# The squares of the first norm: eight instructions between the split parts, or two wide ones behind them

## The chip, the cores and the metric

The kernel runs on one core of a Trainium2 chip. The metric is the device time of one execution in microseconds (us), the median of the runs of a kernel. The core's engines are TensorE (PE; its weight loads are shown apart as PEld), VectorE (DVE), ScalarE (ACT), GpSimd (POOL) and SyncE (SP, which here only issues DMAs). Each takes its instructions in the order in which they were laid down, and waits where an operand is not ready.

## What is computed

One pre-norm layer over x, 512 tokens of 1024 channels, in float32, and a final RMS norm:

```
h    = rmsnorm(x, norm1_g)
proj = h @ w_in                     # parts for four mixers, and four gates of 1024 columns
ys   = gated DeltaNet, RG-LRU, S5, RWKV-7, each from its part of proj
x    = x + (sum_i sigmoid(gate_i) * (ys[i] @ w_branch[i])) @ w_out
h2   = rmsnorm(x, norm2_g)
x    = x + square(relu(h2 @ mlp_w1)) @ mlp_w2
out  = rmsnorm(x, final_norm_g)
```

The part that matters here is the first line: `rmsnorm` divides each token's channels by the root of their mean square (plus 1e-6), times a weight per channel.

## The kernel before

x lies transposed in SBUF: eight chunks of 128 channels by 512 tokens, side by side in one tile `xt` (`xt0`, which fills the region c1b). Its eight loads are issued by SP (line 251) between the raw weights of the first projection and those of the second.

**Products.** A float32 product is done in three matmuls of a reduced format: each operand is split in a high part and the low rest. For x that is `split_g` (line 382), per chunk: ACT scales by the norm's weight and rounds to the high part (line 117), DVE makes the low part (line 129). Weights come in *units* of 128x1024 (`unit`, line 316): the load of `raw` by SP (line 313), the high part by ACT (`hi<-raw`, line 117), the low part by DVE (`lo<-raw,hi`, line 120). Four raw buffers and two of each part are in turn. `gemm` (line 337) then runs 24 matmuls of 128x512 for a unit: for each of the eight chunks high by high, high by low, low by high. The trace calls these `acc<-c,hi` and `acc<-c,lo`.

**The norm.** The projections use x before it is divided; the scale per token, `rsa`, is applied when a projection leaves PSUM (`nproj`, line 419). The scale comes from `norm_stat` (line 345). ACT squares each chunk (`act(sq, xt[k], ACT.Square)`), DVE adds the squares as they come, TensorE sums over the 128 channels of a partition (`ssa`, matmuls with a column of ones), ACT takes the root, DVE the reciprocal, TensorE spreads the result over the partitions (`rsa`), ACT copies it out. The first six projections have a PSUM bank each, so six can be done before one must be scaled.

```
 408          for k in range(8):
 409              split_g(xs[k], "g1", k, xgh[:, k, :], xgl[:, k, :])
 410          N1["rs"] = norm_stat(xs, "a")
 411          fr(xt)
```

**The order of the work.** No order is written out by hand. Each step of a list `PLAN` is emitted at a priority number of its level (`LV`, `level`); units have lower numbers, which rank first, by line 320: `100 * u - (30000 if u else 50000)`. A planner with its own timeline of the kernel (`schedule_with_timeline_sim=True`, line 1816) puts each engine's instructions in line: of those that it holds ready, the one that ranks first. The DMA queue of SP is such a line too. The order is then fixed; the chip only waits.

**Places in SBUF.** Small tiles share five regions: c0 (for the split x), c1a, c1b, c2 and c3. `al` (line 138) gives a tile the place that the table `HOME` names for its name and turn, if that is free at that point of the program; otherwise it searches the free place whose last user was released longest ago. An instruction that writes a tile waits on the chip for the readers of what lay there before.

Other names in the text: `omu` and the activations `c<-pr`, `ea<-pr`, `cl<-pr` prepare constants of the mixers from the parameters `pr` (its second load is line 254); `zero` is a tile of zeros that SP writes eight times to scratch memory (line 432); `wt`, `s5p` and `cb` are a decay table of RWKV, powers for S5 and a constant matrix; `zpg` and `t1pr` are steps of an inversion of triangular blocks in two mixers.

Of the kernel before, what the change touches and what calls it, by code (L numbers as in the profile page):

```python
# [22 lines left out]
HOME = {n: [(a[:a.index(":")], int(a[a.index(":") + 1:])) for a in v.split(",")] for n, v in (e.split("=") for e in """
    xt0=c1b:0 xgh=c0:0 xgl=c0:128 sqa0=c3:650 sqa1=c3:64 sqa2=c3:333 sqa3=c3:618 sqa4=c3:558 sqa5=c1a:81 sqa6=c3:634
    sqa7=c2:185 rsa=c3:202 zero=c2:43,c1b:78 wa=c3:514 gd=c3:64
    px=c2:52,c2:205,c3:383,c3:112,c3:218,c1a:105,c1b:0,c3:488,c3:526,c1b:16,c3:298,c1b:112,c3:525,c1b:16,c2:0,c1b:16
    reset=c3:542 kr=c1b:32 yk=c2:178 svr=c3:0 ab=c2:43 ccb=c1a:59 kf=c3:96,c1a:17 sig=c1b:96,c3:112 af=c3:466,c1b:96
    ei=c1b:112,c1a:0 eia=c1a:80,c3:558 wt=c1a:63,c3:447 bigwup=c3:325 hsbk=c1b:16,c3:298 rf=c3:80,c3:423
    vf=c3:333,c1b:112 rb=c3:349,c3:321 ntr=c1a:64 a2=c3:439 biggup=c2:242 s5s=c3:314 s5pol=c3:134 s5p=c1a:41
    bst=c1a:33 bsx=c2:8 bs2=c3:610 bs3=c3:530 c1=c1a:51 c2=c2:0 bigsb=c3:234 bigsbs=c3:666 bigsc=c2:16 bigscs=c1a:97  # L30
    b8=c3:358 s5t=c3:218,c3:610 s5u=c1a:96 s5ug=c3:325 s5h=c1a:0 lrow=c3:509 gsm=c2:250 ctri=c3:504 qk=c3:96,c3:391
    cv=c1b:0,c3:542,c1b:0,c1b:96,c1a:32,c1a:32 gv=c3:359 lu=c3:542 lh=c1b:96 lr=c1b:0,c1b:16 li=c3:509,c1b:0
    la2=c3:298,c3:298 biglwa=c2:27 biglwx=c2:35 lge=c3:526,c1b:16 c8=c3:218 t8w=c3:138 s5ct=c3:574 s5st=c3:590
    s5am=c2:18 s5ph=c2:175 s5tb=c3:282 s5a=c3:540 s5b=c3:503 s5hs=c3:290 cmr=c3:606 tfr=c2:0 bk=c3:610 s5y=c3:513
    s5yf=c3:326 s5yo=c3:514 bigglu=c1a:48 sgm=c3:290,c3:306 nbr=c1b:87 tnr=c3:128 tmr=c1b:70 tpr=c1b:32 t0tr=c2:210
    ztr=c1b:32 t11tr=c3:574 z2r=c1a:32 ktok=c2:176 ksqg=c1b:64 gpk=c3:136 grows=c3:130 gr=c1a:64 br=c1a:96 eg=c1a:0
    cneg=c2:173 cmg=c2:171 kx=c1b:64 kd=c3:250 svg=c2:176 aq=c3:546 tw=c3:324 ntg=c1a:0 tfg=c3:291 nbg=c1a:40
    tng=c2:35 tmg=c1a:112 tpg=c1a:32 t0tg=c1a:80 ztg=c1a:32 t11tg=c1a:64 z2g=c1a:112
    gt=c1b:0,c1b:0,c1b:16,c3:178,c1b:16,c3:178,c1b:16,c1b:16,c1b:0,c1b:48,c1b:16,c3:185,c1b:16,c1b:16,c3:170,c2:59,c3:234,c1b:0,c3:218,c3:610,c1b:0,c1b:48,c2:75,c2:176,c3:32,c2:0,c3:186,c1b:96,c2:42,c3:513,c1b:16,c2:125,c3:23,c2:32,c3:610,c3:626,c1b:0,c3:580,c3:598,c3:626,c3:337,c3:16,c3:136,c3:64,c3:594,c3:80,c3:626,c3:317
    ofr=c3:128 r1=c3:282,c1b:0,c1b:48,c3:194,c1b:40,c1b:40,c3:505,c1b:40  # L40
    uv=c1b:48,c1b:40,c1b:56,c3:503,c3:168,c3:160,c3:177,c2:34
    sm=c1b:8,c3:194,c1b:40,c3:185,c3:503,c3:168,c3:160,c1b:56 ofg=c2:143
    sn=c3:282,c3:473,c2:117,c3:282,c3:160,c1b:32,c2:92,c3:316
    sgs=c1b:32,c1b:40,c1b:75,c3:315,c3:473,c1b:75,c3:282,c1b:88 osq=c3:658,c3:626 hsbv=c2:16,c3:16 yh1=c1a:32
    yl1=c1a:64 mg=c3:456,c3:497,c3:170,c3:0,c3:48,c3:481,c3:658,c3:234 yh2=c1a:0 yl2=c1a:96 gz=c3:64 q2=c3:530,c1b:112
    o2=c2:240,c3:186 hsbo=c1b:96,c3:513 yh3=c1a:64 yl3=c1a:32 yh0=c1a:96 yl0=c1a:0
    x2=c3:107,c3:642,c3:423,c3:388,c3:407,c3:372,c3:439,c3:290 mh=c2:0 ml=c2:128 h2h=c0:0 h2l=c0:128 sqb0=c3:64
    sqb1=c3:610 sqb2=c3:32 sqb3=c3:0 sqb4=c3:16 sqb5=c3:48 sqb6=c3:531 sqb7=c3:626 rsb=c3:332
    dh=c1a:0,c1b:0,c2:128,c2:0 dl=c2:128,c2:0,c1a:0,c1b:0
    rl=c3:658,c3:0,c3:573,c3:626,c3:20,c3:46,c3:255,c3:0,c3:626,c3:0,c3:594,c3:16,c3:32,c3:56,c3:0,c3:16,c3:16,c3:626,c3:0,c3:32,c3:16,c3:626,c3:156,c3:658,c3:626,c3:610,c3:594,c3:503,c3:626,c3:16,c3:658,c3:0  # L50
    hc0=c3:497 hc1=c3:578 hc2=c3:184 hc3=c3:626 hc4=c3:658 hc5=c3:200 hc6=c3:481 hc7=c3:34 sqc0=c3:513 sqc1=c3:610
    sqc2=c3:236 sqc3=c3:16 sqc4=c3:533 sqc5=c3:610 sqc6=c3:562 sqc7=c3:594 rsc=c3:0
""".split())}
# [47 lines left out]
def trunk(ctx, tc, order, xT, wall, w8, prm, big, cst, gfr, out):  # L101
    nc = tc.nc
    V, A, G, P = nc.vector, nc.scalar, nc.gpsimd, nc.tensor
# [9 lines left out]
    def mm(o, l, r, start=True, stop=True):  # L113
        P.matmul(out=o, lhsT=l, rhs=r, start=start, stop=stop)  # L114

    def act(o, i, f, scale=1.0, bias=0.0):
        A.activation(out=o, in_=i, func=f, scale=scale, bias=bias)  # L117

    def tt(e, o, a, b, op):
        e.tensor_tensor(out=o, in0=a, in1=b, op=op)  # L120
# [99 lines left out]
    def pa(name):  # L220

        n = turn["acc"] = turn.get("acc", -1) + 1
        if n < EARLY or turn.get("late"):
# [4 lines left out]
        return pacc.tile([128, 512], F, tag=f"acc{n % 3}", name=name)


    def v3(t, a):
# [56 lines left out]
    one = const.tile([128, 1], F, name="one")  # L288
    G.memset(one, 1.0)
    ones = bc(one, [128, 128])  # L290
    with priority(-70000):
        o = ps("warm")
# [49 lines left out]
                mm(o, a[:, k0 + k, :], b[:, k, :], first and n == 0, last and n == 3 * nk - 1)  # L342
                n += 1

    def norm_stat(xt, nm, parts=1):

        accs = []
        for k in range(8):
            sq = t2(f"sq{nm}{k}")
# [9 lines left out]
        def keep_warm(n, t):
            if parts > 1:  # L360
                w = pa("warm")
                for _ in range(n):
                    mm(w[:, 0:128], ones, t[:, 0:128])
# [2 lines left out]
        for i, acc in enumerate(accs):
            for u in range(4):
                mm(o[:, u:u + 1], acc[:, u * 128:u * 128 + 128], one, i + u == 0, i == parts - 1 and u == 3)
            keep_warm(3, acc)
        fr(*accs)  # L370
# [1451 lines left out]
```

## Time and profile before

| what | value |
|---|---|
| median of 3 runs | 883.51 us (882.94 to 1213.66) |
| the profiled execution, its own time | 878.68 us |
| its span, first to last instruction | 876.9 us |
| TensorE busy | 855.5 us |
| VectorE busy | 549.2 us |
| ScalarE busy | 422.8 us |
| GpSimd busy | 26.1 us |
| TensorE's granted clock, mean | 0.991 |

All views that follow are of the profiled execution; starts are microseconds from the beginning of its span. A timeline row has start, length, engine, line of the kernel, operation, output and inputs by the program's names, shapes, count, and in brackets the idle time of the engine just before with what ended it. Tiles that lie in a region show as the region's name: `c<-c1b` writes some tile of c and reads x. A wait row has the engine and instruction that waited, what for, the total in us, how often, and the longest. A group row ends with busy time and the mean length in ns, then idle time ahead. Instructions on one engine overlap a little at their ends, so the distance between two starts is what one costs its engine.

### The profile page before, as it was taken

To read this page: it belongs to the slowest core of one execution; us is meant where nothing else is said; L and a number is where in the kernel's file an instruction comes from. 1 tells how busy PE (TensorE), PEld (TensorE's weight loads), DVE (VectorE), ACT (ScalarE), POOL (GpSimd) and SP (SyncE) were. 2 spreads that over 40 slices of the span, in tenths; PEclk is the share of its full clock that TensorE was granted. 3 is DMA by queue.
4 is the path that set the end of the run, shared out by engine and by line. 5 is a ranking of instruction groups with operands and counts; after the bars stand their busy time and mean duration, and the time that the engine had idled before them with its cause. 6 is when DMAs were issued, how large, how long until landed. Compare 5 with 4: busy or idle time off the path is not lost.

```text
span 876.9 us, 12992 instructions
## 1 busy us (share of the span) xinstructions
PE 855.5 (98%) x5175; PEld 688.8 (79%) x5175; DVE 549.2 (63%) x967; ACT 422.8 (48%) x584; POOL 26.1 (3%) x38
## 2 busy tenths in 40 slices
PE   8999999998999899999999999999999999999996
PEld 6777777777777787777888788888888888888885
DVE  6899796993776258636655652454437553868553
ACT  8735557854522273333433333765545443644433
POOL 1000000000000000000000000000100110010000
PEclk9999999999999799999999999999999999999999
DMA  8433345455465652244323232556665877463302
GB/s 296 135 107 110 108 112 116 96 154 150 123 178 151 180 171 73 83 134 117 96 92 102 77 131 96 192 145 173 164 194 159 246 169 200 159 137 104 120 25 96
DMA packets 79292, 119.96 MB, mean 137 GB/s; under 512 B 42544, under 2 KB 49392, under 8 KB 79216
## 3 DMA queue, kind: packets, MB, share of 16 engines
q1 hardware_dynamic: 51968, 100.40, 35.4%
q0 software_dynamic: 3456, 12.58, 8.3%
q10 hardware_dynamic: 23808, 6.16, 3.3%
q8 instruction: 40, 0.66, 0.3%
q14 instruction: 20, 0.16, 0.1%
HBM read 103.79 MB, written 13.17 MB: 133 GB/s over the span
## 4 chain that ended last, share of the span: by engine, by line
PE 79%; DVE 7%; DMA 7%; ACT 4%; issue 2%; SPq 1%; ACTq 0%; DVEq 0%
PE acc L114 24%; PE facc L114 20%; PE dacc L114 17%; PE oacc L114 5%; PE bacc L114 4%; DVE c L120 2%; DMA c1a<-scrg 1%; DVE lo L120 1%; DMA c1a<-gscr 1%; ACT c L117 1%; PE s L114 1%; DMA raw<-in_wall_dram 1%; DVE c L129 1%; ACT L117 1%; DVE c1a L120 1%
## 5 line engine op out<-in xcount | busy, mean ns | idle before, releaser
L114 PE MATMUL acc<-c,hi 128*128 128x512 f32 x864 | 278.3, 400 | 3.7 <-DVE c L129 2.5
L117 ACT ACTIVATE hi<-raw 128x1024 fp32r<-128x1024 f32 x113 | 119.4, 1058 | 239.0 <-PE facc L114 73.5
L120 DVE TENSOR_TENSOR lo<-raw,hi 128x1024 fp32r<-128x1024 f32 x113 | 137.9, 1221 | 118.4 <-ACT hi L117 118.3
L114 PEld LDWEIGHTS acc<-c,hi 128*128 128x128 f32 x864 | 161.6, 190 | 44.4 <-DVE c L129 5.0
L114 PE MATMUL acc<-c,lo 128*128 128x512 f32 x432 | 173.9, 404 | 1.4 <-DVE lo L120 1.4
L114 PE MATMUL facc<-c,hi 128*128 128x512 f32 x336 | 103.4, 389 | 0.0
L114 PEld LDWEIGHTS acc<-c,lo 128*128 128x128 f32 x432 | 81.9, 190 | 20.6 <-DVE lo L120 2.0
L114 PEld LDWEIGHTS facc<-c,hi 128*128 128x128 f32 x336 | 63.1, 188 | 13.1
L117 ACT ACTIVATE c<-c 128x512 f32<-128x512 f32 (+5 forms) x101 | 63.9, 638 | 18.5 <-DVE c L120 11.8
L120 DVE TENSOR_TENSOR c<-c 128x16 f32<-128x16 f32 (+8 forms) x125 | 65.1, 534 | 4.2 <-ACT c L117 3.8
L114 PE MATMUL facc<-c,lo 128*128 128x512 f32 x168 | 65.5, 390 | 0.0
L114 PE MATMUL facc<-c,c1a 128*128 128x512 f32 x264 | 62.8, 391 | 0.0
L114 PE MATMUL dacc<-hi,c 128*128 128x512 f32 x176 | 57.4, 389 | 0.0
L114 PEld LDWEIGHTS facc<-c,c1a 128*128 128x128 f32 x264 | 49.3, 188 | 10.1
L117 ACT ACT_TABLE_LOAD x41 | 52.6, 1283 | 8.5 <-DMA raw<-in_wall_dram 3.0
L120 DVE TENSOR_TENSOR c<-acc,c 128x512 f32<-128x512 f32 x33 | 22.6, 687 | 45.4 <-PE acc L114 45.1
L120 DVE TENSOR_TENSOR c1a<-raw,c1a 128x1024 fp32r<-128x1024 f32 x21 | 25.7, 1223 | 32.7 <-ACT c1a L117 32.6
L114 PE MATMUL bacc<-c1a,hi 128*128 128x512 f32 x128 | 40.6, 401 | 0.0
L114 PE MATMUL oacc<-c,hi 128*128 128x512 f32 x128 | 39.8, 392 | 0.1
L117 ACT ACTIVATE c1a<-raw 128x1024 fp32r<-128x1024 f32 x21 | 22.2, 1058 | 36.5 <-PE facc L114 29.0
L114 PEld LDWEIGHTS dacc<-hi,c 128*128 128x128 f32 x176 | 33.0, 188 | 6.8
L114 PEld LDWEIGHTS facc<-c,lo 128*128 128x128 f32 x168 | 31.5, 188 | 6.5
(390 smaller groups left out, 1194.4 us busy)
## 6 DMA issues: line engine op xcount, KB each, us to landing
raw<-in_wall_dram SPq DMA_DIRECT2D x134, 512.0 KB, 3.5
c<-in_wall_dram POOLq DMA_DIRECT2D x18, 512.0 KB, 5.7
c<-in_wall_dram SPq DMA_DIRECT2D x6, 512.0 KB, 3.5
raw<-in_wall_dram POOLq DMA_DIRECT2D x6, 512.0 KB, 7.1
scg<-c1b SPq DMA_DIRECT2D x11, 256.0 KB, 2.5
c<-scg SPq DMA_DIRECT2D x11, 256.0 KB, 3.6
c1b<-in_xT_dram SPq DMA_DIRECT2D x8, 256.0 KB, 5.2
c<-in_xT_dram SPq DMA_DIRECT2D x8, 256.0 KB, 4.0
```

Of the source, the lines that this page charges most:

```text
L114: P.matmul(out=o, lhsT=l, rhs=r, start=start, stop=stop)
L117: A.activation(out=o, in_=i, func=f, scale=scale, bias=bias)
L120: e.tensor_tensor(out=o, in0=a, in1=b, op=op)
L129: V.scalar_tensor_tensor(out=o, in0=a, scalar=s, in1=b, op0=op0, op1=op1)
```

## The change

`norm_stat` takes the whole tile of x. Two instructions square four chunks each, the even ones (0, 2, 4, 6) and the odd ones, each into a tile of 2048 columns; one addition of 2048 columns joins them, then one of 1024 and one of 512 fold the rest. The four column sums are those of before. The variable number of parts and the optional matmuls around it, unused for this norm, are gone.

```diff
-    def norm_stat(xt, nm, parts=1):
-
-        accs = []
-        for k in range(8):
-            sq = t2(f"sq{nm}{k}")
-            act(sq, xt[k], ACT.Square)
-            if k == 0 or k == 7:
-                accs.append(sq)
-            else:
-                tt(V, accs[-1], accs[-1], sq, ADD)
-                fr(sq)
-        while len(accs) > parts:
-            tt(V, accs[-2], accs[-2], accs[-1], ADD)
-            fr(accs.pop())
...
+    def norm_stat(xt, nm):
+
+
+        sq_ = [t8(f"sw{nm}{e}") for e in range(2)]
+        sq = [v3(t, 4) for t in sq_]
+        for e in range(2):
+            act(sq[e], v3(xt, 8)[:, e:8:2], ACT.Square)
+        tt(V, sq_[0], sq_[0], sq_[1], ADD)
+        fr(sq_[1])
+        for n in (1024, 512):
+            tt(V, sq_[0][:, 0:n], sq_[0][:, 0:n], sq_[0][:, n:2 * n], ADD)
         o = ps("ss" + nm)
...
+        for u in range(4):
+            mm(o[:, u:u + 1], sq_[0][:, u * 128:u * 128 + 128], one, u == 0, u == 3)
+        fr(sq_[0])
...
-        N1["rs"] = norm_stat(xs, "a")
+        N1["rs"] = norm_stat(xt, "a")
```

The table `HOME` is set anew for many small tiles; the wide squares, `swa0` and `swa1`, have no entry in it. The lines of the first tiles (a number counts 32 columns from the region's start):

```diff
-    xt0=c1b:0 xgh=c0:0 xgl=c0:128 sqa0=c3:650 sqa1=c3:64 sqa2=c3:333 sqa3=c3:618 sqa4=c3:558 sqa5=c1a:81 sqa6=c3:634
-    sqa7=c2:185 rsa=c3:202 zero=c2:43,c1b:78 wa=c3:514 gd=c3:64
+    xt0=c1b:0 xgh=c0:0 xgl=c0:128 sqa0=c3:212 sqa1=c3:17 sqa2=c3:250 sqa3=c3:290 sqa4=c1b:57 sqa5=c3:332 sqa6=c3:642
+    sqa7=c1a:4 rsa=c3:202 zero=c1b:96,c1a:31 wa=c3:514 gd=c3:64
...
-    reset=c3:542 kr=c1b:32 yk=c2:178 svr=c3:0 ab=c2:43 ccb=c1a:59 kf=c3:96,c1a:17 sig=c1b:96,c3:112 af=c3:466,c1b:96
+    reset=c3:594 kr=c1b:32 yk=c2:178 svr=c1b:16 ab=c2:43 ccb=c1a:59 kf=c3:96,c1a:17 sig=c3:243,c3:112 af=c3:466,c1b:96
...
-    bst=c1a:33 bsx=c2:8 bs2=c3:610 bs3=c3:530 c1=c1a:51 c2=c2:0 bigsb=c3:234 bigsbs=c3:666 bigsc=c2:16 bigscs=c1a:97
+    bst=c3:191 bsx=c2:8 bs2=c1a:80 bs3=c2:35 c1=c1a:51 c2=c1a:53 bigsb=c3:234 bigsbs=c1b:32 bigsc=c2:16 bigscs=c1a:97
```

The other entries that change are of the mixers, the merge and the MLP. No instruction outside `norm_stat` and its call is changed.

More of the change, by code (lines that the diff above doesn't have):

```diff
@@ L28 @@
-    ei=c1b:112,c1a:0 eia=c1a:80,c3:558 wt=c1a:63,c3:447 bigwup=c3:325 hsbk=c1b:16,c3:298 rf=c3:80,c3:423
-    vf=c3:333,c1b:112 rb=c3:349,c3:321 ntr=c1a:64 a2=c3:439 biggup=c2:242 s5s=c3:314 s5pol=c3:134 s5p=c1a:41
-    bst=c1a:33 bsx=c2:8 bs2=c3:610 bs3=c3:530 c1=c1a:51 c2=c2:0 bigsb=c3:234 bigsbs=c3:666 bigsc=c2:16 bigscs=c1a:97
-    b8=c3:358 s5t=c3:218,c3:610 s5u=c1a:96 s5ug=c3:325 s5h=c1a:0 lrow=c3:509 gsm=c2:250 ctri=c3:504 qk=c3:96,c3:391
-    cv=c1b:0,c3:542,c1b:0,c1b:96,c1a:32,c1a:32 gv=c3:359 lu=c3:542 lh=c1b:96 lr=c1b:0,c1b:16 li=c3:509,c1b:0
@@ L33 @@
[L33 to L37, printed above, removed]
+    reset=c3:594 kr=c1b:32 yk=c2:178 svr=c1b:16 ab=c2:43 ccb=c1a:59 kf=c3:96,c1a:17 sig=c3:243,c3:112 af=c3:466,c1b:96
@@ new lines @@
+    ei=c1b:112,c1a:0 eia=c1a:80,c3:558 wt=c1a:63,c3:447 bigwup=c3:325 hsbk=c1b:16,c3:145 rf=c3:80,c3:423
+    vf=c3:333,c1b:112 rb=c3:349,c3:321 ntr=c1a:64 a2=c1a:89 biggup=c2:242 s5s=c3:314 s5pol=c3:134 s5p=c1a:41
+    bst=c3:191 bsx=c2:8 bs2=c1a:80 bs3=c2:35 c1=c1a:51 c2=c1a:53 bigsb=c3:234 bigsbs=c1b:32 bigsc=c2:16 bigscs=c1a:97
+    b8=c1b:29 s5t=c3:218,c3:610 s5u=c1a:96 s5ug=c3:325 s5h=c1a:0 lrow=c3:509 gsm=c3:128 ctri=c3:612 qk=c3:96,c3:391
+    cv=c1b:0,c3:542,c1b:0,c3:381,c1a:32,c1a:32 gv=c3:359 lu=c3:542 lh=c1b:96 lr=c2:143,c1b:16 li=c3:509,c1b:0
@@ new lines @@
+    la2=c3:298,c3:298 biglwa=c2:27 biglwx=c2:35 lge=c3:526,c1b:16 c8=c3:218 t8w=c1a:84 s5ct=c1b:89 s5st=c3:138
+    s5am=c3:245 s5ph=c1a:98 s5tb=c3:282 s5a=c3:218 s5b=c2:38 s5hs=c3:290 cmr=c3:391 tfr=c3:112 bk=c3:510 s5y=c3:513
+    s5yf=c3:326 s5yo=c3:514 bigglu=c1a:48 sgm=c3:290,c3:306 nbr=c1b:87 tnr=c2:35 tmr=c1b:70 tpr=c1a:76 t0tr=c2:210
+    ztr=c1b:32 t11tr=c3:574 z2r=c1a:32 ktok=c2:176 ksqg=c1b:64 gpk=c1b:83 grows=c3:15 gr=c1a:64 br=c1a:96 eg=c3:387
+    cneg=c3:503 cmg=c1b:112 kx=c1b:64 kd=c3:250 svg=c2:176 aq=c3:546 tw=c3:324 ntg=c1a:0 tfg=c3:291 nbg=c1a:40
@@ L38 @@
     tng=c2:35 tmg=c1a:112 tpg=c1a:32 t0tg=c1a:80 ztg=c1a:32 t11tg=c1a:64 z2g=c1a:112
     gt=c1b:0,c1b:0,c1b:16,c3:178,c1b:16,c3:178,c1b:16,c1b:16,c1b:0,c1b:48,c1b:16,c3:185,c1b:16,c1b:16,c3:170,c2:59,c3:234,c1b:0,c3:218,c3:610,c1b:0,c1b:48,c2:75,c2:176,c3:32,c2:0,c3:186,c1b:96,c2:42,c3:513,c1b:16,c2:125,c3:23,c2:32,c3:610,c3:626,c1b:0,c3:580,c3:598,c3:626,c3:337,c3:16,c3:136,c3:64,c3:594,c3:80,c3:626,c3:317
-    ofr=c3:128 r1=c3:282,c1b:0,c1b:48,c3:194,c1b:40,c1b:40,c3:505,c1b:40
-    uv=c1b:48,c1b:40,c1b:56,c3:503,c3:168,c3:160,c3:177,c2:34
@@ L42 @@
[L42 to L52, printed above, removed]
+    ofr=c3:574 r1=c3:282,c1b:0,c3:306,c3:194,c1b:40,c1b:40,c3:505,c1b:40
@@ new lines @@
+    uv=c1a:8,c1b:40,c1b:56,c3:503,c3:168,c3:160,c3:177,c2:34 sm=c1b:8,c3:194,c1b:40,c2:156,c3:503,c3:168,c3:160,c1b:56
+    ofg=c2:128 sn=c3:282,c2:13,c2:117,c3:282,c3:160,c1b:32,c2:92,c3:316
+    sgs=c1b:32,c1b:40,c1b:75,c3:315,c3:473,c3:466,c3:282,c2:35 osq=c3:658,c3:145 hsbv=c2:16,c3:16 yh1=c1b:70 yl1=c2:16
+    mg=c3:456,c1a:108,c3:45,c1a:40,c3:48,c3:481,c3:481,c3:234 yh2=c3:313 yl2=c3:586 gz=c2:178 q2=c3:530,c1b:112
+    o2=c3:612,c3:32 hsbo=c3:349,c3:321 yh3=c1a:32 yl3=c1b:76 yh0=c2:100 yl0=c1a:84
@@ new lines @@
+    x2=c3:107,c3:391,c3:423,c1a:22,c3:407,c1a:32,c3:439,c3:290 mh=c2:0 ml=c2:128 h2h=c0:0 h2l=c0:128 sqb0=c3:64
+    sqb1=c3:558 sqb2=c1a:32 sqb3=c2:16 sqb4=c3:514 sqb5=c3:447 sqb6=c3:183 sqb7=c3:91 rsb=c3:523
+    dh=c2:193,c3:538,c1a:0,c1b:110 dl=c2:190,c2:0,c3:234,c1b:0
+    rl=c3:658,c3:243,c3:573,c3:626,c3:20,c3:46,c3:255,c3:0,c3:626,c3:250,c3:594,c3:16,c3:32,c3:56,c3:642,c3:16,c3:16,c3:626,c3:0,c3:32,c3:16,c3:626,c3:156,c3:658,c3:626,c3:610,c3:594,c3:503,c3:626,c3:16,c3:658,c1b:20
+    hc0=c3:571 hc1=c3:503 hc2=c3:347 hc3=c1b:56 hc4=c1a:41 hc5=c3:212 hc6=c3:191 hc7=c3:306 sqc0=c3:560 sqc1=c2:193
@@ L53 @@
+    sqc2=c1a:68 sqc3=c1b:6 sqc4=c2:178 sqc5=c2:16 sqc6=c2:22 sqc7=c3:183 rsc=c3:177
 """.split())}
@@ L343, in gemm @@
                 n += 1
-    def norm_stat(xt, nm, parts=1):
-        accs = []
-        for k in range(8):
-            sq = t2(f"sq{nm}{k}")
-            act(sq, xt[k], ACT.Square)
-            if k == 0 or k == 7:
-                accs.append(sq)
-            else:
-                tt(V, accs[-1], accs[-1], sq, ADD)
-                fr(sq)
-        while len(accs) > parts:
-            tt(V, accs[-2], accs[-2], accs[-1], ADD)
-            fr(accs.pop())
[L359 to L363, printed above, removed]
-        o = ps("ss" + nm)
[L366 to L370, printed above, removed]
+    def norm_stat(xt, nm):
[7 more added lines that the diff above has]
+            tt(V, sq_[0][:, 0:n], sq_[0][:, 0:n], sq_[0][:, n:2 * n], ADD)
+        o = ps("ss" + nm)
+        for u in range(4):
+            mm(o[:, u:u + 1], sq_[0][:, u * 128:u * 128 + 128], one, u == 0, u == 3)
+        fr(sq_[0])
         st = sm_.tile([128, 4], F, name="st" + nm)
```

## The prediction

> **What bounds the kernel now.** I read the page first, for the engine that sets the span and the room it leaves, then TensorE's (PE's) idle time by stage.
>
> ```profile
> span 876.9 us, 12992 instructions
> PE 855.5 (98%) x5175; PEld 688.8 (79%) x5175; DVE 549.2 (63%) x967; ACT 422.8 (48%) x584; POOL 26.1 (3%) x38
> ```
>
> TensorE is busy for 855.5 of 876.9 us, so all its idle time is 21.4 us, 2.4% of the span. The stages (columns: length, busy time of PE, weight load, DVE, ACT, POOL, granted clock, DMA share, GB/s):
>
> ```profile
> 7.25:17.73 10.48, 8.00 (x27) 4.38 (x27) 10.48 (x20) 10.45 (x23) 0.00 (x0) 1.00 1.05 387
> 18.80:24.85 6.05, 6.04 (x26) 4.99 (x27) 4.32 (x34) 5.33 (x10) 0.00 (x0) 1.00 0.72 176
> 100.00:200.00 100.00, 96.18 (x800) 74.59 (x799) 85.58 (x221) 63.80 (x85) 0.45 (x2) 1.00 0.48 119
> 200.00:300.00 100.00, 95.43 (x861) 75.78 (x861) 58.01 (x115) 37.10 (x53) 0.00 (x0) 0.93 0.57 160
> 300.00:400.00 100.00, 98.26 (x959) 77.88 (x959) 59.16 (x93) 40.39 (x65) 1.01 (x1) 1.00 0.36 111
> ```
>
> The change works in the first row: 27 matmuls take 10.48 us with ACT and DVE full. From 18.80 on, 26 run in 6.05 us without a gap, about 0.23 us each. At that pace the 24 matmuls of the first projection (unit 0) would need 5.5 us. So unit 0 is paced by ACT and DVE, and that is all the change can win: some 4 us. Who paces it, ACT first (start, length, instruction; hi<-raw is a weight's high part, c<-c1b,pr the high part of an x chunk, c<-c1b a square):
>
> ```profile
> 5.52 1.06 ACT L117 ACTIVATE hi<-raw 128x1024 fp32r<-128x1024 f32 x1 [3.50 <-DMA raw<-in_wall_dram]
> 6.49 0.71 ACT L117 ACTIVATE c<-c1b,pr 128x512 fp32r<-128x512 f32 x1
> 7.10 0.61 ACT L117 ACTIVATE c<-c1b 128x512 f32<-128x512 f32 x1
> 7.62 0.71 ACT L117 ACTIVATE c<-c1b,pr 128x512 fp32r<-128x512 f32 x1
> ...
> 15.04 0.61 ACT L117 ACTIVATE c<-c1b 128x512 f32<-128x512 f32 x1
> 15.56 1.05 ACT L117 ACTIVATE hi<-raw 128x1024 fp32r<-128x1024 f32 x1
> 16.50 0.68 ACT L117 ACTIVATE c<-cs,pr 128x128 f32<-128x128 f32 x2
> 17.09 0.20 ACT L117 ACTIVATE c<-pr 128x16 f32<-128x16 f32 x1
> ```
>
> A high part holds ACT 0.61 us and its square 0.52: 1.13 us a chunk. On DVE a low part (L129) and the addition of a square (L120) alternate:
>
> ```profile
> 6.61 1.23 DVE L120 TENSOR_TENSOR lo<-raw,hi 128x1024 fp32r<-128x1024 f32 x1 [5.24 <-ACT hi L117]
> 7.75 1.41 DVE L129 SCALAR_TENSOR_TENSOR c<-c1b,pr,c 128x512 fp32r<-128x512 f32 x2
> ...
> 14.14 0.23 DVE L126 TENSOR_SCALAR omu<-pr 128x8 f32<-128x8 f32 x2
> ...
> 14.97 0.74 DVE L129 SCALAR_TENSOR_TENSOR c<-c1b,pr,c 128x512 fp32r<-128x512 f32 x1
> 15.63 0.68 DVE L120 TENSOR_TENSOR c<-c 128x512 f32<-128x512 f32 x1
> 16.23 0.74 DVE L129 SCALAR_TENSOR_TENSOR c<-c1b,pr,c 128x512 fp32r<-128x512 f32 x1
> 16.90 0.68 DVE L120 TENSOR_TENSOR c<-c,c 128x512 f32<-128x512 f32 x1
> 17.50 1.22 DVE L120 TENSOR_TENSOR lo<-raw,hi 128x1024 fp32r<-128x1024 f32 x1
> ```
>
> From 14.97 to 16.23 is 1.26 us a chunk, longer than ACT's 1.13: DVE sets the pace, and the last low part of x ends at 16.97. TensorE around that:
>
> ```profile
> 15.77 0.50 PE L114 MATMUL acc<-c,hi 128*128 128x512 f32 x1 [0.52 <-DVE c L129]
> 17.73 0.96 PE L114 MATMUL ssa<-one,c 128*128 128x1 f32 x8
> 18.80 0.73 PE L114 MATMUL acc<-c,hi 128*128 128x512 f32 x2
> ```
>
> So at 18.80 the two weight parts of unit 1 are ready (the low part at 17.50 + 1.22 = 18.72), 26 matmuls are done (24 of unit 0, two of unit 1) and the eight column sums ssa too. From here on TensorE sets the time. The gain is how much earlier it reaches this state.
>
> **The change, part by part.** What is late, once DVE no longer is, depends on when data land:
>
> ```profile
> 1.65 4.20 SPq L251 DMA_DIRECT2D c1b<-in_xT_dram  x8
> 6.17 0.33 SPq L313 DMA_DIRECT2D raw<-in_wall_dram  x1
> 7.51 0.33 SPq L254 DMA_DIRECT2D pr<-in_prm_dram  x1
> 10.92 6.47 SPq L432 DMA_DIRECT2D scrr<-c  x8
> 24.24 0.38 SPq L313 DMA_DIRECT2D raw<-in_wall_dram  x1
> ```
>
> The trace's time to landing is 5.3 us for the last x chunk, whose issue begins at 5.5 (10.8), 6.0 for unit 1's raw weights (12.2) and 5.2 for the parameters pr (12.7).
>
> (a) Squares. Eight of 0.61 us become two over 2048 elements. The trace has no such width, so from these two groups, with DVE's two beside them:
>
> ```profile
> L117 ACT ACTIVATE c<-c1b 128x512 f32<-128x512 f32 x7 | 4.3, 615 | 0.0
> L117 ACT ACTIVATE hi<-raw 128x1024 fp32r<-128x1024 f32 x4 | 4.2, 1054 | 4.1 <-DMA raw<-in_wall_dram 3.5 <-PE acc L114 0.6
> L120 DVE TENSOR_TENSOR lo<-raw,hi 128x1024 fp32r<-128x1024 f32 x3 | 3.7, 1219 | 5.2 <-ACT hi L117 5.2
> L120 DVE TENSOR_TENSOR c<-c 128x512 f32<-128x512 f32 x5 | 3.4, 684 | 0.0
> ```
>
> ACT: 512 more elements cost 0.44 us, so 2048 cost 1.05 + 2 x 0.44 = 1.93 us. The new input is four pieces of 512 with gaps; bounds are 1.93 and, if each piece paid as an instruction does, 4 x 0.61 = 2.44. I take 1.93, the straight line. ACT's squares fall from 4.9 to 3.9 us, which is not the point: they leave the stream of high parts.
>
> (b) Additions. Seven of 0.68 us (4.8) become one each of 2048, 1024 and 512: 1.22 + 2 x 0.535 = 2.29, 1.22 and 0.68, 4.2 us together, all behind the second square. DVE between low parts is free.
>
> (c) The new order. High parts now follow at 0.61 us: number 6 (counted from 0) at 6.49 + 6 x 0.61 = 10.15, ending 10.86. Number 7 waits for its chunk (10.8). The first wide square needs chunks 0, 2, 4 and 6. The planner puts in line what it thinks ready: in the old order a square stood between any two high parts, so it believed the next chunk not yet there. Hence I place the first wide square before the last high part: 10.76 to 12.69. Unit 1's raw is there at 12.2. The old order also tells where its high part will stand. A DVE instruction that reads pr stands in line at 14.14, before the last two low parts, so the planner held pr to have landed by then. Yet the small activations that read only pr (17.09) stand behind unit 1's high part (15.56): had ACT been free in the plan after the last square, with the raw still missing, they would have come first. So in the plan the raw was there by the end of the last square. A unit outranks the norm (its priority number is lower). With ACT now held for 1.93 us by a square just then, unit 1's high part comes right after it or after high part 7, before the second square. Either way both take 12.6 to 14.3, and DVE's two low parts (1.22 and 0.67) end near 15.5, against 18.72.
>
> (d) What TensorE gets. At 15.5 it has done 24 instead of 26 matmuls (two of chunk 7 are open): 2 x 0.23 = 0.45 us. The column sums, 0.96 us in what was a gap, now fall into TensorE's full time. Gain: 18.80 - 15.5 - 0.45 - 0.96 = 1.9 us.
>
> (e) The norm gets later. The second square ends near 16.2, additions at 20.4, against 17.58. Cover: the scale rsa was computed by TensorE only at 24.85 and first read at 28.13, and six accumulators take projections before one must be scaled. Without this cover it costs 2.8 us. I put nothing.
>
> (f) Places. The wide squares have no place in the table, so the search gives them the never-used region c1a, whole. The memsets of wt and s5p and the load of constant cb, which lie in c1a, now wait for the sum; wt is next used at 41.02, cb's matmul comes at 60.28. The zero tile moves into x's place (chunk 6), so its memset and SP's eight scratch writes (10.92) wait for that square, to about 13.0. Queued behind them on SP are constants and the raw load of 24.24, which landed after 3.6 us and was read at 38.25: 10 us to spare, so nothing; uncovered it would be 2.1 us. The other moves change which tile must wait for which. No row prices them. Below, by the idle time of TensorE from 100 to 400 (3.8 + 4.6 + 1.7 = 10.1 us), of which half at best is a place's doing: 5 us gained. Above, by the nearest rows, the longest TensorE waits of the trace:
>
> ```profile
> PE zpg L114 <- DMA c1a<-scrg: 2.6, 2, 1.3
> PE t1pr L114 <- issue: 2.6, 1, 2.6
> ```
>
> two more such waits: 5 us lost. I take zero, between them.
>
> Sum: the profiled execution took 878.68 us, 1.8 beyond its span, so 876.8 for such an execution. The median of the runs shown is 4.8 us higher, 883.51; the same 1.9 off it gives **881.6 us**.
>
> The Trainium skill, Perfetto Trace Analysis, section Optimizing Scalar/DVE Operations, speaks against this change: where ScalarE or VectorE is not saturated but makes another engine wait, it says, breaking instructions up may let work finish sooner. Rows agree as far as high part 7 waits behind 1.93 us of square here; with nothing in front it would stand at 10.8, and the sum would be 3.3 (first rival) in place of 1.9.
>
> **Rivals.**
>
> 1. All high parts and unit 1's go ahead of any square. High part 7 at 10.8, its low part at 7.75 + 7 x 0.67 = 12.4 to 13.1, unit 1's high part 12.2 to 13.25, its low part to 14.5: 18.80 - 14.5 - 0.96 = 3.3, **880.2**. For: the data are there. Against: the planner's old order.
>
> 2. Slower: a parameter read before high part 6. With ACT free between high parts, the planner can slip in the small activations that read pr (17.09), which it believed landed by then. On the chip pr lands at 12.7, and ACT works in order. High part 6 then starts near 13.2, the square ends at 15.7, the last low part of the two at 18.6: 18.80 - 18.6 - 0.45 - 0.96 = -1.2, **884.7**. It decides as soon as such an instruction stands ahead of high part 6; behind number 7 it costs nothing. For: omu at 14.14. Against: squares outrank them, and the planner may see pr only after chunk 6.
>
> 3. The change does not do what it says for TensorE: unit 1's high part stays behind the second square and its low part behind the first addition. Square to 15.2, high part to 16.1, addition 15.2 to 17.4, low part to 18.6, 0.2 us before today, less the 0.96 of ssa: -0.8, **884.3**.
>
> 4. The places decide, by a wait in the mixers: 5 us either way, 876.6 or 886.6 from the forecast.
>
> **How the numbers follow.** Forecast 0.45; first rival 0.12; second 0.15; third 0.15; places 0.13, split evenly. The cases run from 876.6 to 886.6, and the two kinds of reading of before lie 4.8 us apart, so a new reading can lie a little outside: 876.5 to 887.5 holds 8 in 10. The forecast's own range is 880 to 883.5. A measurement of this kernel tells about 2% (17.7 us) from no change. Faster than that would need four fifths of TensorE's 21.4 us of idle time: 0.01. Slower needs a stall seven times the longest seen: 0.02. Within: 0.97.
>
> **What would show it.** Right: low parts of x at a pitch near 0.67, not 1.26; the first wide square of 1.9 us ahead of the last high part; unit 1's high part before the second square; TensorE unbroken from about 15.5; ssa near 20.5. Wrong: ACT waiting for pr ahead of high part 6 (rival 2); unit 1's high part behind both squares (3); a wide square of 2.4 us; new TensorE waits above 1 us after 100 us (4); or, with all steps as forecast, a span that does not shrink: then a later chain and not TensorE's work carries the end.

## The result, and the profile after

The changed kernel takes 893.12 us (median of 5 runs, 888.76 to 894.41), the kernel before 882.94 us in 5 runs beside it. A run far above all others of its kernel (1213.66 us of before here; one run each of d_s5u, d_gv and d_lu below) is left out of the ratios and of the medians in the table. The ratio is 1.0127, with a 95% interval of 1.0092 to 1.0163: slower by about 1.3%. The forecast was 881.6 us, with a range of 876.5 to 887.5, so the time lies outside, on the far side of every rival that had a price.

The profiled execution took 893.3 us (878.68 before). The head of its page:

```profile
span 891.5 us, 12973 instructions
PE 864.6 (97%) x5175; PEld 696.5 (78%) x5175; DVE 548.8 (62%) x963; ACT 418.4 (47%) x575; POOL 26.3 (3%) x38
```

The span grew by 14.6 us. TensorE has the same 5175 matmuls as before and is busy 9.1 us longer with them; its idle time grew from 21.4 to 26.9 us, by 5.5 (2.0 more in the first 25 us, 4.7 more from 150 to 350, 1.2 less from 350 to 500). 9.1 + 5.5 is the whole growth. Where each lies, by stage (columns as in the windows of before):

```profile
7.25:17.73 10.48, 6.86 (x25) 4.42 (x25) 8.22 (x14) 10.25 (x16) 0.31 (x1) 1.00 1.04 388
...
18.00:19.00 1.00, 0.91 (x3) 0.52 (x4) 1.00 (x5) 0.43 (x5) 0.00 (x0) 0.67 0.91 304
19.00:20.00 1.00, 1.00 (x4) 0.81 (x4) 1.00 (x1) 0.98 (x3) 0.00 (x0) 0.50 0.82 274
...
25.00:150.00 125.00, 125.00 (x657) 94.41 (x657) 110.24 (x324) 66.18 (x91) 0.00 (x0) 1.00 0.32 97
...
150.00:350.00 200.00, 186.41 (x1969) 149.26 (x1966) 120.44 (x243) 91.57 (x135) 2.26 (x3) 0.92 0.53 140
```

The same two stretches of before, where the clock matters:

```profile
25.00:150.00 125.00, 125.00 (x661) 95.45 (x660) 110.86 (x294) 68.79 (x93) 2.13 (x2) 1.00 0.40 112
150.00:350.00 200.00, 191.12 (x2039) 152.31 (x2039) 133.26 (x277) 94.80 (x140) 0.13 (x1) 0.97 0.51 143
```

Three things are to be seen. From 25 to 150 us both kernels keep TensorE full at full clock. From 150 to 350 us, where the four mixers' small products run between projections, after has 4.7 us more idle time, and the granted clock falls from 0.97 to 0.92. And around 19 us after has a stretch at half clock that before lacks. The first product of the merge tells how much was lost by then, first in before, then in after:

```profile
L114 PE MATMUL oacc<-c,hi x128: 389/389/497, 489.0 to 534.9; 128*128 128x512 f32 x128
```

```profile
L113 PE MATMUL oacc<-c,hi x128: 387/389/497, 503.6 to 549.4; 128*128 128x512 f32 x128
```

It starts 14.6 us later, which is all of the growth: the rest of the kernel is alike. The first stage accounts for 1.6 us of this (next). The other 13.0 are put down to the mixers by subtraction, since TensorE is full at full clock in between.

**The first stage.** ACT's line in after (the rows answer to the high parts and squares of before):

```profile
8.31 2.74 ACT L116 ACTIVATE c<-c1b,pr 128x512 fp32r<-128x512 f32 x4 [0.23 <-DMA c1b<-in_xT_dram]
10.96 1.90 ACT L116 ACTIVATE c1a<-c1b 128x2048 f32<-128x2048 f32 x1
12.76 0.70 ACT L116 ACTIVATE c<-c1b,pr 128x512 fp32r<-128x512 f32 x1
13.37 1.90 ACT L116 ACTIVATE c1a<-c1b 128x2048 f32<-128x2048 f32 x1
15.17 1.04 ACT L116 ACTIVATE hi<-raw 128x1024 fp32r<-128x1024 f32 x1
```

and DVE's:

```profile
7.20 4.72 DVE L128 SCALAR_TENSOR_TENSOR c<-c1b,pr,c 128x512 fp32r<-128x512 f32 x7
...
13.49 0.75 DVE L128 SCALAR_TENSOR_TENSOR c<-c1b,pr,c 128x512 fp32r<-128x512 f32 x1 [0.23 <-ACT c L116]
15.30 2.29 DVE L119 TENSOR_TENSOR c1a<-c1a 128x2048 f32<-128x2048 f32 x1 [1.05 <-ACT c1a L116]
17.51 1.22 DVE L119 TENSOR_TENSOR lo<-raw,hi 128x1024 fp32r<-128x1024 f32 x1
```

The pitch of the low parts is 0.67 us, as forecast, and the first wide square stands ahead of the last high part, at 10.96 (10.76 forecast). But unit 1's high part stands behind the second square, at 15.17, and its low part behind the wide addition, at 17.51: no earlier than the 17.50 of before. TensorE:

```profile
14.64 0.40 PE L113 MATMUL acc<-c,lo 128*128 128x512 f32 x1
16.26 0.73 PE L113 MATMUL acc<-c,hi 128*128 128x512 f32 x2 [1.23 <-ACT hi L116]
18.09 1.03 PE L113 MATMUL acc<-c,hi 128*128 128x512 f32 x2 [1.10 <-ACT hi L116]
18.92 0.66 PE L113 MATMUL acc<-c,lo 128*128 128x512 f32 x1
...
26.41 0.95 PE L113 MATMUL ssa<-one,c1a 128*128 128x1 f32 x8
```

Unit 0 is done at 15.0. Then come 3.1 us with two matmuls in them, and after these the clock is halved: the single matmul at 18.92 takes 0.66 us in place of 0.40, and pairs start every 1.28 us (19.37, 20.65) in place of 0.68. It is back to full before 22. Wide products begun by 25 us, in before:

```profile
L114 PE MATMUL acc<-c,hi x35: 387/396/504, 7.2 to 24.6; 128*128 128x512 f32 x35
L114 PE MATMUL acc<-c,lo x17: 389/393/402, 8.9 to 24.4; 128*128 128x512 f32 x17
```

in after:

```profile
L113 PE MATMUL acc<-c,hi x34: 389/394/628, 6.7 to 24.8; 128*128 128x512 f32 x34
L113 PE MATMUL acc<-c,lo x15: 388/395/656, 8.3 to 24.4; 128*128 128x512 f32 x15
```

52 against 49, and after has its column sums still ahead: 3 x 0.23 + 0.96 = 1.6 us behind. This is in spite of an earlier start: the first product began at 6.69 us in after and at 7.25 in before. The start moves from execution to execution (6.61 to 6.87 us in e_keep, d_s5u, d_gv and d_lu below, whose first stage is that of before), so up to half a microsecond of such a comparison is not the change's.

**The mixers.** TensorE's longest waits of after beyond the first stage, and one stretch with what follows it:

```profile
PE zpr L113 <- issue: 3.4, 1, 3.4
PE vtT L877 <- DVE egl L854: 2.9, 1, 2.9
...
PE zpg L113 <- DMA c1a<-scrg: 1.6, 1, 1.6
```

```profile
210.00:213.00 3.00, 0.00 (x0) 0.00 (x0) 0.00 (x0) 0.00 (x0) 0.00 (x0) 0.98 0.94 325
213.00:227.00 14.00, 13.73 (x239) 12.77 (x239) 4.19 (x7) 3.31 (x8) 0.00 (x0) 0.52 0.13 46
```

After three empty microseconds (while the DMA engines are 94% busy) TensorE works for 14 us at half clock. The trace names nothing that the last `zpr` matmuls waited for ("issue"). They read what was loaded from scratch, with issues from 201.8 us on, so a late landing is likely, but not shown. I added the halved time of whole kernels from windows of 1 us, as the sum of 2 x (1 - granted clock) over those with a clock under 0.9, up to 6 us before the end: 13.6 us before, 33.8 after. Half of the difference, 10.1 us, is the most that it can add to TensorE's busy time; 9.1 were added.

### The profile page after: what moved, and what is told of

It is laid out like the page before. It is cut to its first block, busy times and chain, and to the rows that moved or that the text cites. A ratio compares the mean times of both kernels' runs of the same rounds, so it can differ in the third digit from the quotient of the medians.

```text
span 891.5 us, 12973 instructions
## 1 busy us (share of the span) xinstructions
PE 864.6 (97%) x5175; PEld 696.5 (78%) x5175; DVE 548.8 (62%) x963; ACT 418.4 (47%) x575; POOL 26.3 (3%) x38
## 4 chain that ended last, share of the span: by engine, by line
PE 84%; DMA 5%; DVE 4%; ACT 4%; issue 2%; SPq 1%; POOL 0%; ACTq 0%; DVEq 0%; POOLq 0%
PE acc L113 26%; PE facc L113 20%; PE dacc L113 17%; PE bacc L113 5%; PE oacc L113 5%; DMA c1a<-scrg 1%; PE s L113 1%; ACT c L116 1%; PE s5y L113 1%; DMA c<-scrr 1%; ACT L116 1%; DVE c L128 1%; DVE c1a L119 1%; ACT hi L116 1%; DMA c1b<-in_xT_dram 1%
## 5 line engine op out<-in xcount | busy, mean ns | idle before, releaser
L113 PE MATMUL acc<-c,hi 128*128 128x512 f32 x864 | 281.9, 405 | 5.0 <-ACT hi L116 2.7
L113 PEld LDWEIGHTS acc<-c,hi 128*128 128x128 f32 x864 | 164.4, 192 | 46.0 <-issue 4.9
L113 PEld LDWEIGHTS acc<-c,lo 128*128 128x128 f32 x432 | 83.3, 193 | 20.7 <-DVE lo L119 1.6
L119 DVE TENSOR_TENSOR c<-c 128x16 f32<-128x16 f32 (+8 forms) x118 | 59.7, 522 | 2.0 <-ACT c L116 1.5
L113 PEld LDWEIGHTS facc<-c,c1a 128*128 128x128 f32 x264 | 49.3, 188 | 10.1
L113 PE MATMUL dacc<-hi,c 128*128 128x512 f32 x160 | 52.7, 389 | 0.0
L113 PE MATMUL dacc<-hi,c1b 128*128 128x512 f32 x112 | 37.1, 389 | 0.0
```

## The experiments

Three theories were set against each other. **A, order and clock:** any edit makes the planner lay the mixers out anew. What is lost is pauses that the new order has there, and the halved clock that follows a pause; the table HOME suits one order. **B, the late scale:** the scale `rsa` is copied at 33.4 instead of 25.9 us, and all that depends on it slides by that much. **C, the places alone:** the new places make small tiles wait for one another, whatever the order.

All that was measured, so that the parts below can refer to it (rsa: when its second half is copied; idle: span less TensorE's busy time):

| run | median us | ratio to before, 95% | rsa | PE busy | idle | half clock |
|---|---|---|---|---|---|---|
| before | 880 to 883 | | 25.9 | 855.5 | 21.4 | 13.6 |
| after | 893.12 | 1.0127 (1.0092 to 1.0163) | 33.4 | 864.6 | 26.9 | 33.8 |
| e_squares | 897.62 | 1.0206 (1.0168 to 1.0244) | 34.5 | 867.2 | 27.3 | 44.1 |
| e_places | 941.50 | 1.0701 (1.0657 to 1.0745) | 30.9 | 871.5 | 68.0 | 85.2 |
| e_sqplaces | 895.34 | 1.0170 (1.0134 to 1.0206) | 31.3 | 863.3 | 29.3 | 34.1 |
| e_warm | 888.00 | 1.0098 (1.0059 to 1.0137) | 35.2 | 862.5 | 21.7 | 27.2 |
| e_delay | 891.53 | 1.0144 (1.0104 to 1.0184) | 40.1 | 857.9 | 32.5 | 23.5 |
| e_late | 889.29 | 1.0086 (1.0054 to 1.0118) | 36.1 | 856.4 | 29.8 | 23.7 |
| e_raw1 | 885.14 | 1.0046 (1.0023 to 1.0069) | 33.8 | 858.0 | 24.2 | 27.3 |
| b_raw1 | 890.91 | 1.0121 (1.0092 to 1.0149) | 29.8 | 861.4 | 26.7 | 30.3 |
| e_keep | 884.22 | 1.0053 (1.0032 to 1.0075) | 25.4 | 862.1 | 20.7 | 6.7 |
| d_s5u | 899.52 | 1.0218 (1.0183 to 1.0253) | 25.4 | 860.2 | 37.5 | 47.6 |
| d_gv | 885.52 | 1.0060 (1.0038 to 1.0083) | 25.5 | 859.5 | 24.2 | 23.7 |
| d_lu | 882.96 | 1.0035 (1.0016 to 1.0054) | 25.3 | 859.7 | 22.3 | 27.3 |

### The two halves of the change

e_squares is the changed code with the table of before; e_places is the code of before with the changed table.

```diff
 e_squares (against after), e_places the other way round (against before)
-    xt0=c1b:0 xgh=c0:0 xgl=c0:128 sqa0=c3:212 sqa1=c3:17 sqa2=c3:250 sqa3=c3:290 sqa4=c1b:57 sqa5=c3:332 sqa6=c3:642
+    xt0=c1b:0 xgh=c0:0 xgl=c0:128 sqa0=c3:650 sqa1=c3:64 sqa2=c3:333 sqa3=c3:618 sqa4=c3:558 sqa5=c1a:81 sqa6=c3:634
...
```

> Wide squares with the table of places of before. Theory A (order and clock): what costs is the new order of the work in the mixers, in which TensorE meets pauses of some 3 us and its clock is then granted at half for 3 to 14 us; the first 25 us themselves cost at most 2 us. The order is new here too, so the time may lie anywhere from 879 to 895 us, and its distance to before should equal, within 2 us, the growth of TensorE's idle time plus half of the growth of the half-clock stretches. Theory B (late scale): the norm's scale, 7 us later with the wide squares, moves every mixer by as much: 889 to 893 us, whatever the clock does. Theory C (places alone): 880 to 883 us.

> Narrow squares of before with the new table of places. Theory A: again a new order in the mixers, 879 to 895 us, with the loss in pauses and half-clock stretches there. Theory B (late scale): the scale is as late as the squares make it; if the first column sums come at about 18 us as before, 880 to 884 us. Theory C (the new places make false waits): 889 to 893 us.

The squares alone: +2.06%, 897.62 us, outside the range of every theory. Nor did A's sum hold within its 2 us: 5.9 us of idle time and half of 30.5 us of half clock make 21.2, and the span grew by 17.6. Half of the half-clock time is only the most that it can cost, since some of it falls where TensorE waits anyway. The places alone: +7.0%, far beyond what was expected. Two waits make up 23.8 us of e_places' 46.6 us of added idle time, and the mixers' stage shows the rest and the clock:

```profile
PE bkT L659 <- ACT c L660: 11.9, 1, 11.9
PE r L113 <- DVE c L119: 11.9, 1, 11.9
```

The first of these can be read. On ACT's line the issue of a load from scratch (L469, at 228.71 us) stands ahead of the copy of `bkT` (L660, at 229.36) that frees the PSUM tile for TensorE. ACT did nothing for the 8.3 us ahead of that copy, and the trace puts them down to ACT's own writes to scratch (L465, issued from 223.16), behind which that load comes. The trace thus points to the order of ACT's line, not to a place.

```profile
150.00:350.00 200.00, 149.52 (x1625) 116.84 (x1624) 108.17 (x256) 78.77 (x114) 2.25 (x3) 0.79 0.41 100
```

So the halves do not add up. The changed table loses 7% with the old squares, yet with the new ones it is better than the old table (1.27% against 2.06%; the intervals just fail to overlap). Theory C falls in its form "whatever the order": a table is not good or bad by itself, it fits an order or does not. The squares cost +2.06% with the old table and +1.27% with the table that came with them; whether a table set with more care for them would give less was not tried.

### The places of the eight squares alone

The changed table names places for `sqa0` to `sqa7`, which the changed kernel no longer has. e_sqplaces gives the kernel before those eight and nothing else.

```diff
-    sqa0=c3:650 sqa1=c3:64 sqa2=c3:333 sqa3=c3:618 sqa4=c3:558 sqa5=c1a:81 sqa6=c3:634 sqa7=c2:185
+    sqa0=c3:212 sqa1=c3:17 sqa2=c3:250 sqa3=c3:290 sqa4=c1b:57 sqa5=c3:332 sqa6=c3:642 sqa7=c1a:4
```

> The kernel before with other places for the eight small square tiles alone; no instruction is added or taken away, but the planner's order of the rest comes out otherwise. Theory A (the order of the mixers is a draw, and before was a good one): the time leaves that of before by 3 to 15 us, slower, and the difference is TensorE's idle time and half-clock stretches between 150 and 350 us. Theory B (late scale): only as far as the scale is later (first column sums and rsa as in before: 0 to 2 us; if rsa comes 4 us later: 4 us).

+1.7%, or 15.4 us, just beyond the 3 to 15 of theory A. The scale comes only 5.4 us later than in before. Tiles that are dead by 25 us cost most of it after 150 us:

```profile
150.00:350.00 200.00, 183.03 (x1956) 146.27 (x1955) 123.09 (x266) 95.09 (x136) 0.13 (x1) 0.92 0.50 137
```

### The clock in the first stage

e_warm adds four matmuls of 128x512, whose result nobody reads, to the changed kernel; they need the wide squares, and most of them fall into the gap at 15 us (the trace shows the four as eight instructions: two at 12.79 us, six from 15.20).

```diff
+        w = ps("wm")
+        for i in range(4):
+            mm(w, ones, sq_[i % 2][:, 512:1024])
         tt(V, sq_[0], sq_[0], sq_[1], ADD)
```

> The changed kernel with four matmuls of 128x512 added, which read the wide squares and whose result nothing reads; they fill TensorE's gap between the first two projections (15 to 18 us). If that gap is what halves the clock from 18.7 to 21.8 us: granted clock 1.00 in all of the first 25 us, and TensorE as far as in the changed kernel 1 to 1.5 us earlier at 25 us. If the clock falls for another reason: the same half-clock stretch. The total is 2 us lower if nothing else moves, but the order of the mixers may be new (885 to 893 us).

```profile
15.20 2.84 PE L114 MATMUL wm<-c1a,one 128*128 128x512 f32 x6 [0.28 <-ACT c1a L117]
...
18.35 0.40 PE L114 MATMUL acc<-c,lo 128*128 128x512 f32 x1
```

```profile
L114 PE MATMUL acc<-c,hi x38: 387/389/799, 6.8 to 25.0; 128*128 128x512 f32 x38
L114 PE MATMUL acc<-c,lo x18: 388/389/398, 8.4 to 24.5; 128*128 128x512 f32 x18
```

The matmul that took 0.66 us takes 0.40 again, and 56 wide products are begun by 25 us instead of 49: seven of 0.23, 1.6 us, although TensorE has more to do. With the column sums (0.96) still ahead, that is level with before. The halved clock was thus what the first stage lost; without it the squares' rearrangement gives and costs nothing, but for the start, which was 0.46 us earlier here than in before. The rest of the +0.98% is the mixers' again.

### The late scale

e_delay leaves the squares as before and sends the norm's result to memory and back twice before it is spread out.

```diff
         V.reciprocal(out=st, in_=st)
+        for i in range(2):
+            far = dram.tile([128, 4], F, name=f"far{i}")
+            nc.sync.dma_start(out=far, in_=st)
+            st = sm_.tile([128, 4], F, name=f"st{nm}{i}")
+            nc.sync.dma_start(out=st, in_=far)
```

> The kernel before, in which the norm's scale is written to DRAM and read back twice before it is used, so that it comes some 8 to 10 us later, as in the changed kernel, with squares and places of before. Theory B (late scale): 890 to 893 us. Theory A: the delay is covered by six accumulators and by projections that do not need it; the time is that of a new order, 880 to 888 us, and below 886 most likely.

891.53 us: the time that theory B gave came true, and A's figure did not. The trace says how: TensorE itself stood still,

```profile
PE rsa L114 <- DMA sta<-far: 3.8, 1, 3.8
```

and 3.3 us at half clock followed. That is at most 3.8 + 1.7 = 5.5 of the 13.5 us of span, and the rest is in the mixers. So a scale that TensorE has to wait for costs that wait; this run does not decide about the remainder. e_late does it without the DMAs, by giving the whole norm a late rank:

```diff
-        N1["rs"] = norm_stat(xs, "a")
+        with priority(2500000):
+            N1["rs"] = norm_stat(xs, "a")
```

> The kernel before with the whole computation of the norm's scale ranked behind the first mixers' steps, so that the second half of the scale comes some 4 to 5 us later without any instruction added. Theory B: 4 to 5 us slower. Theory A: a new draw, anywhere from 880 to 895 us.

The scale's second half comes at 36.1 us, later than in after, and the time is +0.86%, less than after's. Theory B's figure of 4 to 5 us was wrong here too: 9.3 us were lost. From 25 to 150 us no time was lost at all; from 150 on, much:

```profile
25.00:150.00 125.00, 125.00 (x658) 94.08 (x657) 109.16 (x272) 69.43 (x94) 2.12 (x2) 1.00 0.36 108
150.00:350.00 200.00, 181.32 (x1992) 143.34 (x1991) 125.66 (x282) 92.48 (x135) 0.13 (x1) 0.94 0.54 141
```

### One entry of the table

If A is right, a single place in the mixers must move the time while the first stage stays as it is. Three kernels, each the one before with one entry changed:

```diff
 d_s5u
-    s5u=c1a:96
+    s5u=c3:558
 d_gv
-    gv=c3:359
+    gv=c3:130
 d_lu
-    lu=c3:542
+    lu=c3:170
```

> The kernel before with one entry of the table of places changed: the S5 input tile s5u lies elsewhere. No instruction is added, and TensorE's line is the same up to its 113th row, well behind the norm's scale, which comes as early as in before. Theory A (a table fitted to one order; any other order is a worse draw): slower by 2 to 15 us, with the loss in idle time and half-clock stretches between 150 and 350 us. Theory B (late scale): the same as before within 1.5 us.

> The kernel before with one other entry changed: the DeltaNet value tile gv lies elsewhere; TensorE's line is the same up to row 354, the scale as early as in before. Theory A: slower by 2 to 15 us. Theory B: the same as before within 1.5 us.

> The kernel before with one other entry changed: the RG-LRU tile lu lies elsewhere; TensorE's line is the same up to row 354, the scale as early as in before. Theory A: slower by 2 to 15 us. Theory B: the same as before within 1.5 us.

They cost 2.2%, 0.6% and 0.35%, with the scale no later than before in all three. The order did change: in before TensorE does the second eight matmuls of `bkT` at 154.2 us, ahead of `ktT` at 159.5; in d_gv and d_lu `ktT` stands first (158.4 and 157.7) and those of `bkT` come last at 179.8 and 179.5. In d_s5u the first difference is at 66 us: one `lg` matmul stands ahead of `al` and `wl` there, in before three. For d_s5u, the scale, the stretch that lost most, and its two longest waits from 150 to 350 us:

```profile
L379 ACT COPY c<-rsa x2: 373/373/373, 25.0 to 25.4; 128x256 f32<-128x256 f32 x2
```

```profile
240.00:290.00 50.00, 32.36 (x628) 26.51 (x627) 28.94 (x58) 15.07 (x24) 0.00 (x0) 0.59 0.54 112
```

```profile
PE us L114 <- DVE c L685: 5.8, 1, 5.8
PE vtT L889 <- DVE c L120: 4.3, 2, 3.3
```

Theory B falls as the cause: 19 us are lost with an early scale, and the latest scale of all runs (40.1) is not the slowest. Theory A holds in kind; its size, which was put at 2 to 15 us, was too small at the upper end. An entry changes the place and, through the planner, the order; which of the two makes a given wait these runs do not separate.

### The first stage in another order

e_raw1 is the changed kernel with unit 1's raw weights loaded ahead of the last three chunks of x; b_raw1 is the kernel before with the same edit.

```diff
-    with priority(-40000):
-        for k in range(8):
+    for k in range(8):
+        with priority(10 * k - 40000):
             nc.sync.dma_start(out=xs[k], in_=xT[k])
...
-                raw = load(key)
+                with priority(-39955 if u == 1 else tc.cur_priority):
+                    raw = load(key)
```

> The changed kernel with the raw weights of the second projection loaded ahead of the last three chunks of x, so that their high part stands ahead of both wide squares. If the gap between the first two projections is what TensorE loses in the first stage: no pause above 1 us and granted clock 1.00 in the first 50 us, TensorE about 3.5 us further at 50 us than in the changed kernel. What the mixers then lose is a new draw: 880 to 893 us.

> The kernel before, narrow squares and old places, with the raw weights of the second projection loaded ahead of the last three chunks of x. The first stage gains what the order allows: with the weight's high part ahead of the last squares TensorE has other matmuls while it waits for low parts of x, 2 to 3.5 us by 25 us. In the total theory A puts a new draw of the mixers on top, 878 to 892 us; theory B, with the scale about as early as in before, 877 to 881 us.

```profile
L113 PE MATMUL acc<-c,hi x44: 387/391/502, 7.0 to 24.7; 128*128 128x512 f32 x44
L113 PE MATMUL acc<-c,lo x21: 388/389/506, 8.6 to 25.0; 128*128 128x512 f32 x21
```

With the weights there in time, e_raw1 begins 65 wide products by 25 us: 16 more than after (3.7 us), 13 more than before. Less the column sums that is 13 x 0.23 - 0.96 = 2.0 us gained on before, the size of the gain that the prediction gave to this stage. And yet the kernel is 0.46% slower than before, for in the mixers TensorE is busy for 188.34 us of the 200 (191.12 before), and at a clock of 0.93 (0.97):

```profile
150.00:350.00 200.00, 188.34 (x2003) 150.58 (x2002) 122.52 (x241) 89.66 (x133) 2.25 (x3) 0.93 0.55 146
```

b_raw1 has 60 by 25 us, ahead of before by 8 x 0.23 = 1.8 us (2 to 3.5 expected), and is 1.2% slower with a scale only 3.9 us later: a gain in the first stage is given back many times over. Against each other, e_raw1 is the quicker of the two by 0.7%, so with this order of loads the wide squares are not worse than the narrow ones; by theory A a difference of this size is no proof for them either.

### Keeping the clock up in the mixers

e_keep adds 24 matmuls of 128x128 at the lowest rank ahead of each block inversion in the kernel before, into an unused half of a PSUM tile.

```diff
+        with priority(90000000):
+            for i in range(24):
+                mm(v3(zp[:, 256:384], 2), ones, nt[:, 2 * (i % 8):2 * (i % 8) + 2, :])
```

> The kernel before with 24 small matmuls added ahead of each of the two block inversions, in the pause in which TensorE waits for a DMA there (287 to 291 us in before); nothing reads their results. Clock theory: the half-clock stretch of 10.2 us that follows that pause is gone or shorter, the time 2 to 5 us less than before if the rest of the order holds. If the halved clock there costs nothing, since the stage waits for other engines: same as before, within 1.5 us. A new order of the mixers can add 3 to 15 us to either.

The half clock fell from 13.6 to 6.7 us and the time still rose by 0.5%: with the added matmuls (96 instructions in the trace, two for each) TensorE's busy time rose by 6.6 us. But they did not land where they were meant to. Those for the first inversion run between 160 and 225 us, those for the second from 259.6 to 265.7, and the pause within the second one's own work, from 292.6 us, is empty, and longer than the two of 1.3 us there in before:

```profile
PE zpg L115 <- issue: 4.4, 1, 4.4
```

So this run decides nothing about keeping the clock up. It too laid the mixers out anew, and that alone may be why less time was halved.

## Why the prediction was wrong

- **Durations (a, b) were right.** A wide square took 1.90 us (1.93 forecast), the additions 2.29, 1.22 and 0.68, as forecast; four pieces with gaps cost no more than one.
- **The order (c) was half right.** The pitch and the first square were right. The failed step is the inference that the planner held unit 1's raw weights to have landed by the end of the old last square, so that their high part would go ahead of the second wide square. It went behind, and the low part behind the addition. That is the third rival's order (chance 0.15), which gave -0.8 us. Its reckoning fits as far as it goes: TensorE had 26 products done at 18.09 us, 0.71 ahead of before, of which 0.56 is the earlier start and 0.15 the change (0.2 forecast). Where the planner's own clock puts a landing does not follow from the order alone.
- **The gain of 1.9 us (d) was a loss of 1.6.** The 0.96 us of column sums came as reckoned. What the sum had no term for is the clock: the two matmuls between 15.0 and 18.1 us were counted as a wait, when they were also the cause of 3.4 us at half rate, 1.7 us. With e_warm the loss is gone. With e_raw1, which has another order of loads, 2.0 us are gained; that it matches the 1.9 is no proof of the steps in between.
- **The late norm (e) at nothing was right** in after: TensorE has no gap from 25 to 150 us. e_delay shows its price when the cover is gone, 3.8 us of wait.
- **The places (f) are the term that was mis-sized, and the larger failure:** zero taken, 5 us either way as bounds, against 13.0 us measured for the new places and the new order together. Pricing the places by the two longest waits of before was the error, and the sum had no term at all for a new order of the mixers. Those waits belong to an order that is laid out anew by every edit, so the rows of before bound nothing. One entry costs 2.4 us (882.96 less its before, 880.61) to 18.9 (899.52 less 880.61), the table alone 61 (941.50 less 880.08). Nor did the bound hold the halved clock that follows a pause, although the prediction's own row for 200 to 300 us shows a clock of 0.93. The fourth rival had the place right ("a wait in the mixers") and little more than a third of the size.
- **The rule that speaks against the change does not settle it.** What the prediction quotes from the Trainium skill, Perfetto Trace Analysis, section Optimizing Scalar/DVE Operations, is for an engine that is not saturated. ACT was busy for 10.45 of the 10.48 us of unit 0 in before (10.25 in after). That high part 7 waited behind a square came true (12.76 us), but that wait is not what cost the 13 us.
- **The last doubt did not arise:** no later chain carries the end; TensorE's lost time does.

What stays open: how the 13 us split between the new order and the new places, which single entries of the changed table cost it, and how much a table set anew for this order would give back. No version here beats the kernel before.

## What to carry to other kernels

Where a planner lays out the work, an edit of 2 us in the first stage is also a new order for all that follows: measure how far neutral changes (a single place, a rank) move the time, 2 to 19 us here, and credit an edit only beyond that. Count TensorE's clock in the sum: a pause of some 3 us costs its length and again up to half of the slow stretch behind it, while the six short waits in the first stage of before, 2.5 us together and the longest 0.81, cost only themselves.

## What the runs showed of the hardware

The granted clock falls to exactly half, in stretches that are multiples of about 3.4 us: in after 3.4 us at 18.4, 3.4 at 185.7, 13.6 at 212.9, 6.8 at 298.2, 3.4 at 311.9 and 3.4 at 329.0. These starts lie on one grid: they are 49, 8, 25, 4 and 5 steps of 3.41 us apart. The two falls of before, at 201.7 and 290.5, are 26 such steps apart, on a grid that lies otherwise against the program. So the clock is decided step by step, and where a pause falls among the steps matters: the one at 180.4 to 183.3 us straddles two, and the clock falls 2.4 us after it has ended.

The step ahead of a fall need not be idle. In the 3.41 us ahead of the six falls of after TensorE was busy for 1.1, 1.6, 0.4, 1.8, 2.3 and 1.9 us, while one step with 1.6 us kept the full clock. Nor does any work end the slow stretch. TensorE was busy throughout in the slow steps from 216.3 and 219.8 us, with 83 and 143 matmuls, most of them 16 or 64 columns wide, and the next step was slow again; after a busy step with 9 to 45 matmuls the clock rose each time. The Trainium skill, TensorE: Matmul & The Clock Gate, section Part 1: The HAM clock gate (the "warmup" mystery), tells of half rate after an idle window of about 3.4 us, of a window that runs freely, and of full rate after about 3.4 us of sustained work. The length of the steps and the grid agree; that a stretch of small matmuls kept the clock down four windows long goes beyond it, and which share of busy cycles counts as work no run here settles.
